# Two calls of the gate products round their weights' first part on ScalarE instead of GpSimd

## The chip, the cores and the metric

The kernel runs on one core of a Trainium2 chip, as one program with one launch. The metric is the time on the device in microseconds, the median of several executions. Five queues of instructions run beside each other: TensorE (PE, with its weight loads listed as PEld), VectorE (DVE), ScalarE (ACT), GpSimd (POOL) and SyncE (SP), which issues most of the DMAs.

## The reference, cut to what matters

One layer over 2048 latent tokens and 256 context tokens of width 1024. A modulated RMSNorm gives `h`; one input projection of it feeds two token mixers and the gates that multiply and merge what they give.

```python
h = _rmsnorm(x, norm_w) * (1.0 + scale[:, None]) + shift[:, None]
w_state, w_rest = w_in[:, :N_STATE], w_in[:, N_STATE:]
qkv, beta_r, decay_r, kb, vb = _split_cols(h @ w_state, STATE_SIZES)
za, qb, zb, ga, gb = _split_cols(h @ w_rest, REST_SIZES)   # za, zb: 512 columns; ga, gb: 1024
oa, _, _ = _gdn_bidir(qa, ka, va, g, bt, s_f, s_b, True)   # gated DeltaNet, both directions
ya = _gdn_output(oa, za, gdn_norm_w)                       # rmsnorm(oa) * silu(za)
ob = _latent_attention(...)                                # window of 128, 8 heads
yb = ob * jax.nn.silu(zb)
y = jax.nn.sigmoid(ga) * (ya @ w_proj_a) + jax.nn.sigmoid(gb) * (yb @ w_proj_b)
x = x + gate[:, None] * (y @ w_out)
```

The DeltaNet runs in chunks of a state recurrence, for each head, forwards and backwards:

```python
v_new = u_n - jnp.einsum('bhck,bhkv->bhcv', w_n, s)
s_new = s * jnp.exp(gl_n)[..., None, None] + jnp.einsum('bhck,bhcv->bhkv', kd_n, v_new)
o = jnp.einsum('bhck,bhkv->bhcv', qd_n, s) + jnp.einsum('bhij,bhjv->bhiv', qk_n, v_new)
```

## The kernel before, in words

All arithmetic is in float32. Where a product is large, each operand is split in two parts: a high part rounded to the format `fp32r`, and a low part, the rest that the rounding left. Three matmuls (L524 to L526: high by high, high by low, low by high) then make one product of nearly full precision. The high and low parts of `h` (`hh`, `hl`) stay in SBUF for a group of 512 tokens; there are four latent groups.

The gates `za`, `zb`, `ga`, `gb` have 24 feature tiles of 128 columns. `gates` (L824) goes through a list of tiles and, for each, through a list of token groups. For a tile, `weights` (L235) loads 1024 x 128 weights in two halves of 256 KB (`wr`, two buffers), makes the high part `wh` of each half with one cast of 128 x 512, and the low part `wl` with one subtraction on DVE (L246). The cast is made either by POOL (L245) or, with `by_act`, by ACT (L243). `wh` and `wl` have two buffers each, so a cast can be done once the last product that reads the tile two places before has run. A tile and a token group are 24 matmuls of 128 x 128 by 128 x 512 into one of three accumulators (`rps`), evicted by a tanh on ACT (L810) and, for `za` and `zb`, by one more product on DVE (L812), and stored. The next tile's weights are asked for after the first token group of the tile in hand (L831).

There are three places of such work. All 24 tiles of token groups 2 and 3 come first, with the casts on ACT (L838). The first 15 tiles of groups 1 and 0 (`BESIDE` = 15) run beside the scan: four tiles are written ahead of it (L1164) and eleven behind it (L1167). The last nine tiles of groups 1 and 0 come after the attention and keep their casts on POOL.

The scan (`scan`, L1060) has 18 steps, each for both directions. In a step, `chain` makes the product of the state with the keys (`ksps`, L1085), corrects `x` (L1087), multiplies by the merged triangular matrix (`vps`, L1091), scales on DVE (`v`, L1094) and updates the state by `sps` (L1103) with L1106 in the first step and L1109 later. `merge` (L976) prepares the matrix of the next step: transposes (`mtp`), a copy on ACT (L1011), products (`myp`, `mep`) and copies on ACT (L1019, L1025, L1026) into `mw`, `my` and `mx`, whose empty parts POOL clears (L984). `output` (L1114) makes `aps` (L1126) and `ops` (L1137) and combines them on DVE (L1134 or L1131, L1138); the direction that comes to a block second loads what the first stored (`osp`). `finalize` (L1038) normalizes the sum and multiplies it by the gate. On DVE the long solution of triangular blocks in `base` (L690 to L762) ends in the same stretch, and a last one, `base4` (L764), follows it in the same buffer `N`: loaded in part by DMA (L777), scaled (L779), copied into three more ranges of partitions by DMA (L784), and solved by 63 pairs of small operations (L789, L791), which stand in DVE's queue among those of the scan.

What sets the order: the program is written in Python loops, but a scheduler with a simulated timeline (`schedule_with_timeline_sim=True`) sorts the instructions of each engine, and the scan has a higher priority than what is written around it (L1165). Each engine then runs its own list in that order, and waits by semaphores. So the list of PE is one sequence of gate matmuls with the products of the scan set between them. From 898 us on the stretch is that of the fifteen tiles; their last products, the scan's last steps and the first attention blocks share the time up to about 1410 us.

Of the kernel before, what the change touches and what calls it, by code (L numbers as in the profile page):

```python
# [32 lines left out]
def hybrid(tc, ins, out, dbg=None, upto=9):  # L33
    nc = tc.nc
    V, S, G, T = nc.vector, nc.scalar, nc.gpsimd, nc.tensor
    ctx = ExitStack()
    with ctx:
        _hybrid(ctx, tc, nc, V, S, G, T, ins, out, dbg, upto)


def _hybrid(ctx, tc, nc, V, S, G, T, ins, out, dbg, upto):
# [9 lines left out]
    def mem(tag):  # L51
        if dbg is not None:
            print("MEM", tag, tile.free_sbuf_bytes_per_partition(tc))
# [744 lines left out]
    def rest(ev, m, by_act):  # L798

        col, dst, mm = ((C_ZA, zasp, m) if m < 4 else (C_ZB, zbsp, m - 4) if m < 8 else  # L800
                        (C_GA, gasp, m - 8) if m < 16 else (C_GB, gbsp, m - 16))
        w = weights(w_in[:, col + mm * 128:col + mm * 128 + 128], KT, by_act)
        return w, dst, mm

    def rest_run(ev, job, m, gi):
        w, dst, mm = job
        ps = acc([128, 512], name="rps")
        fm_dense(ps, w, hh[gi], hl[gi])
        t = ev.tile([128, 512], F32, name="rt", bufs=2)
        S.activation(t, ps, AF.Tanh, scale=0.5)  # L810
        if m < 8:
            V.scalar_tensor_tensor(t, t, 1.0, ps, op0=ALU.add, op1=ALU.mult)  # L812
        (dma if m < 8 else adma)(dst[gi][mm], t)

    BESIDE = 15
# [8 lines left out]
    def gates(ms, gis, beside=(), by_act=False):  # L824
        beside = iter(beside)
        job = rest(ev, ms[0], by_act)
        for i, m in enumerate(ms):
            for j, gi in enumerate(gis):
                rest_run(ev, job, m, gi)
                if j == 0:  # L830
                    nxt = rest(ev, ms[i + 1], by_act) if i + 1 < len(ms) else None  # L831
                    next(beside, None)
            job = nxt
# [195 lines left out]
    def scan_consts(pool):  # L1029
        gw = pool.tile([128, 1], F32, name="gw")  # L1030
        dma(gw, ins["gdn_norm_w"][0].rearrange("(p o) -> p o", o=1))
        V.tensor_scalar(gw, gw, 0.5, None, op0=ALU.mult)
        al2 = pool.tile([128, NB, H], F32, name="al2")
        V.tensor_tensor(al2, alpha, alpha, op=ALU.mult)
        V.tensor_scalar(al2, al2, 1.0 / 128, None, op0=ALU.mult)
        return gw, al2
# [123 lines left out]
    with tc.tile_pool(name="scan", bufs=1, side="right", reuse_waits="tile") as scp:  # L1160
        scl_ = tc.tile_pool(name="scan2", bufs=1, reuse_waits="tile")
        scl = scl_.__enter__()
        cs = scan_consts(scl)
        gates(list(range(4)), (1, 0))  # L1164
        with tc.high_priority(tc.cur_priority):  # L1165
            scan(scp, scl, cs)
        gates(list(range(4, BESIDE)), (1, 0))  # L1167
        mem("r1b")
        scl_.__exit__(None, None, None)
    bs2_.__exit__(None, None, None)  # L1170
# [196 lines left out]
```

## Time and profile before

| | |
|---|---|
| time, median of 3 runs (lowest to highest) | 2026.38 us (2021.74 to 2027.2) |
| the profiled execution | 2024.6 us |
| its span, first to last instruction | 2022.9 us |
| mean granted TensorE clock | 0.986 |
| busy share PE, DVE, ACT, POOL | 96%, 70%, 39%, 32% |
| gate matmuls (L524 to L526 on `rps`) | 768 each, 308.4 to 308.6 us each line |
| casts of weights on POOL (L245) | 72, 47.7 us |
| subtractions L246 on DVE | 120, 92.6 us |

All rows are of one profiled execution. A row of the timeline gives the start in microseconds from the span's start, the duration, the engine, the line of the program, the operation, its output and inputs with their shapes, and in brackets the time for which the engine had stood idle, with what released it. A row of the waits adds up such idle times for one line and one releaser. In the table by stretch each engine has its busy time and its count of instructions, and after POOL come the granted clock (1.00 is 2.4 GHz), the mean busy share of the DMA engines and what they moved in GB/s.

### The profile page before, as it was taken

How to read it: one execution, taken by the hardware profiler on the slowest of the kernel's cores; microseconds unless marked ns; L12 is line 12 of the kernel's file. 1: busy time of each engine (PE TensorE's matmuls, PEld its weight loads, DVE VectorE, ACT ScalarE, POOL GpSimd, SP SyncE). 2: the span in 40 equal slices, each digit the busy share in tenths (PEclk: the TensorE clock that was granted, in tenths of full speed). 3: DMA queues.
4: the chain of work that ended last, by engine and by line, in shares of the span. 5: the costliest groups of instructions: out<-in, count | busy, mean ns of one | idle time of the engine just before them, and what ended most of it. 6: DMA issues, size and time to landing. Idle time of an engine off the chain costs nothing. (4 is left out here: it accounts for less than half of the span.)

```text
span 2022.9 us, 32038 instructions
## 1 busy us (share of the span) xinstructions
PE 1943.7 (96%) x11043; PEld 1630.9 (81%) x11043; DVE 1413.3 (70%) x2774; ACT 786.9 (39%) x1975; POOL 656.8 (32%) x751
## 2 busy tenths in 40 slices
PE   6999999989999899999999999999989999999999
PEld 3888888779898778787788888878777888878887
DVE  7979766667776999999699556635676878743322
ACT  6755545554343322111122223325665656531100
POOL 1742210224542211004222234323555443442221
PEclk8999999999999999999999999999999999999999
DMA  7552326755447633528877777664455555365542
GB/s 259 168 138 85 95 88 159 198 151 163 143 144 190 164 115 109 144 86 234 206 222 213 219 230 218 196 190 156 146 167 173 183 161 169 113 190 181 181 146 94
DMA packets 375511, 333.11 MB, mean 165 GB/s; under 512 B 83833, under 2 KB 299185, under 8 KB 374709
## 3 DMA queue, kind: packets, MB, share of 16 engines
q1 hardware_dynamic: 347924, 288.59, 49.4%
q10 hardware_dynamic: 27424, 42.48, 5.9%
q8 instruction: 87, 1.43, 0.3%
q14 instruction: 76, 0.61, 0.1%
HBM read 220.28 MB, written 109.13 MB: 163 GB/s over the span
## 5 line engine op out<-in xcount | busy, mean ns | idle before, releaser
L524 PE MATMUL rps<-hh,wh 128*128 128x512 f32 x768 | 308.4, 402 | 6.4 <-DVE rt L812 5.1
L526 PE MATMUL rps<-hh,wl 128*128 128x512 f32 x768 | 308.6, 402 | 0.0
L525 PE MATMUL rps<-hl,wh 128*128 128x512 f32 x768 | 308.5, 402 | 0.0
L524 PEld LDWEIGHTS rps<-hh,wh 128*128 128x128 f32 x768 | 145.4, 189 | 41.8 <-DVE rt L812 5.5
L563 DVE SCALAR_TENSOR_TENSOR cacc<-y,cw,cacc 128x512 f32<-128x512 f32 (+1 forms) x224 | 162.3, 746 | 22.7 <-ACT cacc L561 18.6
L524 PE MATMUL lps<-hh,wh 128*128 128x512 f32 (+1 forms) x448 | 171.5, 383 | 0.3 <-ACT y L634 0.3
L525 PEld LDWEIGHTS rps<-hl,wh 128*128 128x128 f32 x768 | 145.4, 189 | 32.4
L526 PE MATMUL lps<-hh,wl 128*128 128x512 f32 (+1 forms) x448 | 171.4, 382 | 0.0
L526 PEld LDWEIGHTS rps<-hh,wl 128*128 128x128 f32 x768 | 145.4, 189 | 32.0
L525 PE MATMUL lps<-hl,wh 128*128 128x512 f32 (+1 forms) x448 | 171.2, 382 | 0.0
L938 DVE TENSOR_TENSOR pl<-pt,ph 128x512 fp32r<-128x512 f32 x156 | 105.4, 685 | 43.7 <-ACT ph L936 42.9
L936 ACT CAST ph<-pt 128x512 fp32r<-128x512 f32 x156 | 90.4, 585 | 112.2 <-PE pt L934 77.8
L910 DVE CUSTOM_DVE_ANT_0 pr<-sc,band,sk 128x640 f32<-128x640 f32 (+1 forms) x128 | 106.5, 862 | 33.8 <-PE sc L906 18.1
L810 ACT ACTIVATE rt<-rps 128x512 f32<-128x512 f32 x96 | 57.3, 597 | 176.2 <-PE rps L526 162.6
L749 DVE TENSOR_TENSOR N<-N,btmp 128x62 f32<-128x62 f32 (+30 forms) x124 | 116.8, 942 | 3.0
L920 POOL TENSOR_SCALAR pr<-pr,sm 128x640 f32<-128x640 f32 (+1 forms) x128 | 99.7, 800 | 56.5 <-DVE sm L918 40.9
L747 DVE TENSOR_TENSOR btmp<-N 128x62 f32<-128x62 f32 (+30 forms) x124 | 114.8, 926 | 3.1
L912 ACT ACTIVATE pr<-pr,sm 128x640 f32<-128x640 f32 (+1 forms) x128 | 104.0, 815 | 19.6 <-DVE sm L910 19.6
L1216 PE MATMUL pps<-yh,wph 128*128 128x512 f32 x256 | 105.2, 415 | 5.8 <-ACT yh L1198 4.3
L246 DVE TENSOR_TENSOR wl<-wr,wh 128x512 fp32r<-128x512 f32 x120 | 92.6, 787 | 24.6 <-POOL wh L245 22.3
L245 POOL TENSOR_SCALAR wh<-wr 128x512 fp32r<-128x512 f32 x72 | 47.7, 678 | 180.1 <-PE lps L525 97.1
L1217 PE MATMUL pps<-yl,wph 128*128 128x512 f32 x256 | 101.5, 397 | 0.0
(301 smaller groups left out, 4944.9 us busy)
## 6 DMA issues: line engine op xcount, KB each, us to landing
wr<-in_w_in_dram SPq DMA_DIRECT2D x120, 256.0 KB
kw<-Ksp SPq DMA_DIRECT2D x28, 384.0 KB
x<-vsp SPq DMA_DIRECT2D x36, 256.0 KB
k<-ksp SPq DMA_DIRECT2D x34, 256.0 KB
kT<-kTsp SPq DMA_DIRECT2D x34, 256.0 KB
wm<-in_w_mod_dram SPq DMA_DIRECT2D x16, 512.0 KB
xt<-in_x_dram SPq DMA_DIRECT2D x16, 512.0 KB
dtl<-Dsp SPq DMA_DIRECT2D x32, 256.0 KB
```

The lines of the kernel that those rows point to most:

```text
L524: T.matmul(ps, lhsT=wh[:, k], rhs=xh[:, k], start=k == 0, stop=False)
L525: T.matmul(ps, lhsT=wh[:, k], rhs=xl[:, k], start=False, stop=False)
L526: T.matmul(ps, lhsT=wl[:, k], rhs=xh[:, k], start=False, stop=k == kt - 1)
L563: V.scalar_tensor_tensor(a, y[:, t:t + n], cw[:, m, t:t + 1], a, op0=ALU.mult, op1=ALU.add)
L747: V.tensor_tensor(tv, A[:, m + 1:, m].unsqueeze(2).to_broadcast([h1 + n, r, m]), A[:, m, 0:m].unsqueeze(1).to_broadcast([h1 + n, r, m]), o ...
L749: V.tensor_tensor(A[:, m + 1:, 0:m], A[:, m + 1:, 0:m], tv, op=ALU.add)
L910: V.tensor_tensor_reduce(s_, ps[:, o:768], band[:, b0:b0 + W + 256], -0.125, sk[:, 1, hd:hd + 1], ALU.add, ALU.min, sm[:, h, 1:2])
L912: S.activation(s_, s_, AF.Exp, scale=-1.0, bias=sm[:, h, 1:2], accum_out=sm[:, h, 2:3])
L920: G.tensor_scalar(p[:, h, :W + 256], p[:, h, :W + 256], sm[:, h, 3:4], 1.0, op0=ALU.mult, op1=ALU.mult)
L938: V.tensor_tensor(pl, pt, f32(ph), op=ALU.subtract)
L1216: T.matmul(ps, lhsT=wh[:, k, ms], rhs=hs[k], start=k == 0, stop=False)
L1217: T.matmul(ps, lhsT=wh[:, k, ms], rhs=ls[k], start=False, stop=False)
```

## The change

The two calls of `gates` around the scan pass `by_act=True`. Nothing else is changed. In `weights` (quoted above) this takes the branch L243 instead of L245 for 15 tiles, two casts each.

```diff
         cs = scan_consts(scl)
-        gates(list(range(4)), (1, 0))
+        gates(list(range(4)), (1, 0), by_act=True)
         with tc.high_priority(tc.cur_priority):
             scan(scp, scl, cs)
-        gates(list(range(4, BESIDE)), (1, 0))
+        gates(list(range(4, BESIDE)), (1, 0), by_act=True)
```

Since the scheduler sorts by its own timeline, the lists of all engines are another order afterwards. Three places follow. The first is ACT's list at the scan's start, as a difference of the two lists (`+` is new); `rt` is the gate's eviction, `mw`, `my` and `mx` are the parts of the merged matrix for the second step.

```order
 L810 ACTIVATE rt<-rps 128x512 x2
 L1011 COPY mw<-mtp 128x512
+L243 CAST wh<-wr 128x512 x2
 L1019 COPY my_10262<-myp 64x256
+L243 CAST wh<-wr 128x512 x2
 L1025 ACTIVATE mw<-mep 64x4x64
 L1026 ACTIVATE mx_10246<-mep 64x4x64
 L810 ACTIVATE rt<-rps 128x512
 L1011 COPY mw<-mtp 128x512
+L243 CAST wh<-wr 128x512 x2
```

Two pairs of casts now stand among the copies of one merge, the second of them directly ahead of L1025, and the third pair behind the next merge's first copy.

The second place is DVE's list where the solution of `base4` (L789 and L791 by turns) and an early output of the scan (`oa_10561`, L1138) stand together, again as a difference.

```order
 L789 TENSOR_TENSOR btmp<-N,btmp 128x61
 L791 TENSOR_TENSOR btmp<-btmp 128x61
+L1138 TENSOR_TENSOR oa_10561<-ops,oa_10561 128x512
 L789 TENSOR_TENSOR btmp<-N,btmp 128x60
 L791 TENSOR_TENSOR btmp<-btmp 128x60
 L789 TENSOR_TENSOR btmp<-N,btmp 128x118
-L1138 TENSOR_TENSOR oa_10561<-ops,oa_10561 128x512
 L791 TENSOR_TENSOR btmp<-btmp 128x59x2
```

L1138 has moved ahead of three of the small products.

The third place is PE's list at the first product of the scan that reads a state (L1085 on `S_10219`), in the order before,

```order
 L1103 MATMUL sps<-v_10231,k_10221 128x128 x4
 L1016 MATMUL myp<-my_10262,moff_10250 64x64
 L1014 MATMUL myp<-mw,moff_10244 64x64
...
 L526 MATMUL rps<-hh_150,wl 128x512
 L524 MATMUL rps<-hh_150,wh 128x512
 L525 MATMUL rps<-hl_151,wh 128x512
...
 L1085 MATMUL ksps<-S_10219,kT_10295 128x128 x4
```

and in the order after:

```order
 L1016 MATMUL myp<-my_10262,moff_10250 64x64
 L1085 MATMUL ksps<-S_10219,kT_10295 128x128 x4
 L526 MATMUL rps<-hh_150,wl 128x512
 L524 MATMUL rps<-hh_150,wh 128x512
 L525 MATMUL rps<-hl_151,wh 128x512
```

Before, 21 gate matmuls stood between the last of the small products `myp` and L1085; now they stand behind L1085, so that 100 instead of 121 gate matmuls of the changed tiles are ahead of it.

## Rows read from the trace of the kernel before

**Rows 1.** the page's first part: engine, busy us, share of the span, instructions.

```profile
PE 1943.7 (96%) x11043; PEld 1630.9 (81%) x11043; DVE 1413.3 (70%) x2774; ACT 786.9 (39%) x1975; POOL 656.8 (32%) x751
```

**Rows 2.** table by stretch, 900 to 1220: length, engines, clock, DMA.

```profile
900.00:1220.00 320.00, 308.30 (x2174) 264.60 (x2173) 242.90 (x542) 70.36 (x203) 97.23 (x135) 0.98 0.76 215
```

**Rows 3.** PE's waits from 900 to 1410: total us, times, longest.

```profile
PE ksps L1085 <- DVE S L1109: 5.4, 2, 4.7
PE aps L1126 <- DVE oa L1138: 3.2, 1, 3.2
PE ops L1137 <- DVE oa L1131: 2.0, 1, 2.0
PE sps L1103 <- DVE v L1094: 1.8, 2, 1.3
PE rps L524 <- ACT rt L810: 1.3, 3, 0.7
PE fps L1055 <- DVE oa L1048: 0.5, 1, 0.5
```

**Rows 4.** DVE's timeline before 992: start, us, instruction, [idle <-releaser].

```profile
966.22 0.11 DVE L756 MEMSET N<- 128x64 f32 x1
986.81 4.41 DVE L779 TENSOR_TENSOR N<-N,btmp 32x4096 f32<-32x4096 f32 x1 [10.72 <-DMA N<-Nsp]
```

**Rows 5.** DVE's timeline, 1014 to 1017.

```profile
1014.37 0.26 DVE L789 TENSOR_TENSOR btmp<-N,btmp 128x63 f32<-128x63 f32 x1 [5.71 <-DMA N<-N]
1016.42 0.26 DVE L791 TENSOR_TENSOR btmp<-btmp 128x60 f32<-128x60 f32 x1
1016.71 0.28 DVE L789 TENSOR_TENSOR btmp<-N,btmp 128x118 f32<-128x118 f32 x1
```

**Rows 6.** DVE's timeline near 1173.

```profile
1173.45 1.13 DVE L1131 SCALAR_TENSOR_TENSOR oa<-aps,npre,oa 128x128 f32<-128x128 f32 x4 [6.41 <-DMA oa<-osp]
```

**Rows 7.** lines of cast and subtraction (min/median/max ns); L246, 897 to 1380.

```profile
L245 POOL TENSOR_SCALAR wh<-wr x72: 614/622/1222, 135.0 to 1404.4; 128x512 fp32r<-128x512 f32 x72
L243 ACT CAST wh<-wr x48: 603/619/623, 568.9 to 887.3; 128x512 fp32r<-128x512 f32 x48
L246 DVE TENSOR_TENSOR wl<-wr,wh x120: 673/684/1786, 135.8 to 1405.5; 128x512 fp32r<-128x512 f32 x120
L246 DVE TENSOR_TENSOR wl<-wr,wh 128x512 fp32r<-128x512 f32 x44 | 35.3, 819 | 17.4 <-POOL wh L245 17.4
```

**Rows 8.** PE's timeline of gate matmuls, first and last of ten.

```profile
902.67 0.40 PE L526 MATMUL rps<-hh,wl 128*128 128x512 f32 x1
...
904.77 0.40 PE L526 MATMUL rps<-hh,wl 128*128 128x512 f32 x1
```

**Rows 9.** PE's timeline at scan products, and DVE's first state copy.

```profile
947.85 1.28 PE L1085 MATMUL ksps<-S,kT 128*128 128x128 f32 x10
954.74 1.06 PE L1091 MATMUL vps<-x,mw 128*128 128x128 f32 x8
1017.77 2.08 PE L1126 MATMUL aps<-S,qT 128*128 128x128 f32 x8 [3.25 <-DVE oa L1138]
943.46 0.69 DVE L1106 COPY S<-sps 128x512 f32<-128x512 f32 x1
```

**Rows 10.** the table by stretch, slices of 10 us.

```profile
990.00:1000.00 10.00, 5.30 (x36) 4.53 (x34) 9.97 (x14) 0.76 (x2) 5.14 (x4) 0.69 0.53 147
1010.00:1020.00 10.00, 6.75 (x53) 6.08 (x52) 5.29 (x20) 0.37 (x1) 0.83 (x1) 0.89 0.97 265
1170.00:1180.00 10.00, 8.02 (x49) 6.57 (x48) 3.77 (x11) 3.08 (x13) 2.97 (x5) 0.83 0.83 241
```

**Rows 11.** timelines of POOL and ACT near 949, and POOL at 1019.

```profile
948.86 0.69 POOL L245 TENSOR_SCALAR wh<-wr 128x512 fp32r<-128x512 f32 x1 [1.08 <-DMA wr<-in_w_in_dram]
949.83 0.38 ACT L1025 ACTIVATE mw<-mep 64x256 f32<-64x256 f32 x1 [6.49 <-PE mep L1023]
1019.16 2.17 POOL L1078 TENSOR_TENSOR x<-x,rin 128x512 f32<-128x512 f32 x2 [11.46 <-DMA x<-vsp]
```

## The prediction, made before the changed kernel was run

> **What bounds the kernel now.** I read the page's shares first: TensorE (PE) is busy 96% of a span of 2022.9 us, the next engine, VectorE (DVE), 70% [rows 1]. So a change elsewhere counts only through PE's idle time. The change acts from the first gate of token groups 0 and 1, near 898 us, to the end of the fifteenth tile; after that a sorted order of gates, scan and first attention blocks ends near 1410. The table by stretch comes next: in the 320 us from 900 to 1220 PE is busy 308.3, DVE 242.9, ScalarE (ACT) 70.4 and GpSimd (POOL) 97.2 [rows 2]. ACT and POOL are both mostly idle there. Then PE's waits: from 900 to 1410 there are 14.2 us of them in all, 12.9 of those end on DVE, 1.3 on ACT's evictions; POOL and the casts are in none [rows 3]. Three waits make up most of it: 4.7, 3.25 and 2.0 us [rows 3, 9]. Last the timeline around these three. In the first, DVE stood 10.72 us before L779 until the load of N landed, ran L779 for 4.4 us, and only then came to the state update L1109 for which PE stood at L1085 [rows 4]. In the second DVE stood 5.71 us for the copy of N into the other partitions, then ran nine small products before L1138 [rows 5]. In the third it stood 6.41 us for the output that the other direction had stored (L1131) [rows 6]. All three are DVE's own queue behind a DMA.
>
> **The change part by part.** It takes 30 casts (15 tiles of two) off POOL and gives them to ACT. On POOL one takes 0.622 us (median), on ACT 0.619 [rows 7]: 18.7 us leave POOL, 18.6 us come to ACT.
> *POOL, minus 18.7 us.* What hides it is PE's own work: no PE wait of the stretch ends on POOL. The nearest is the 0.5 us before L1055, whose last releaser is DVE's L1048, itself fed by POOL [rows 3]. I take 0; the bound is a gain of 0.5.
> *ACT, plus 18.6 us.* The cast of a tile waits for the last product that reads the buffer of two tiles before, as it did on POOL, and in the new order each pair stands where that product has just been issued, mostly next to the eviction of the same group, which becomes ready one matmul later. A pair is 1.24 us. The eviction it delays has three accumulators ahead of it, that is two groups of 24 gate matmuls, and one matmul takes 2.10 us / 9 = 0.233 us [rows 8], so 11 us. The scan's copies behind a pair are needed 4 us or more later, which one place of the rivals below spells out. I take 0; without that cover a pair costs its 1.24 us, 18.6 in all, which no row comes near.
> *DVE.* The subtraction L246 that follows each cast averages 0.819 us in this stretch against a median of 0.684 overall, and stood 17.4 us for POOL's cast [rows 7]. If the difference were POOL's doing, 30 x 0.135 = 4.1 us of DVE work go. Most of that lies in DVE's idle time. It can reach the end only ahead of the first stall, where DVE is full up to the MEMSET L756 at 966.22, behind which N is stored and the next N loaded into its buffer [rows 4]. But there the tail of DVE's list waits for PE: the scan's first products L1103 have 96 gate matmuls ahead of them in both orders, so the state updates before L756 cannot move far. I take 0.7 us earlier, between 0 and 4.1.
> The Trainium skill (SBUF — State Buffer, section Who interferes with whom) says that a VectorE instruction with two SBUF inputs and a GpSimd one that reads SBUF lock each other out, while ScalarE waits for nobody. The 0.819 against 0.684 agrees with it; taken to its end the rule would give all of the 4.1 us to DVE, and 2020.5 if every bit of it counted. The rows above let only the 0.7 through.
> *Order.* The sorted order changes on every engine, and that is where the time can move. PE's total work is the same, so I count how many gate matmuls stand ahead of each of the three waiting products, from the first matmul of the changed tiles. Ahead of the L1085 of the first stall: 227 before, 229 now: 2 x 0.233 = 0.5 us of that wait is filled. DVE's list from L1012 to L1109 has the same instructions. From there to the L1126 of the second: 28 before, 29 now, 0.2 us; and DVE reaches L1138 behind six small products instead of nine, two of the three that it no longer waits for taking 0.26 and 0.28, so 0.8 us sooner [rows 5]: 1.0 us gained. Between the store and the reload of the third: 21 before, 19 now, so its wait grows by 0.5 us. A new narrow place is the first L1085 of the scan, with 100 gate matmuls ahead instead of 121: PE comes there near 947.85 - 4.9 = 942.9, and the state that it reads was copied at 943.46, behind a subtraction that now stands after the copy [rows 9]. It may wait half a microsecond, which only takes as much from the 4.7 us behind it.
> Sum: -0.7 - 0.5 - 1.0 + 0.5 = -1.7 us. The profiled execution took 2024.6 us (1.7 outside its span), so 2022.9 on its scale; it lies 1.8 under the median of the runs, 2026.4, on whose scale the sum gives 2024.7. I forecast 2024.
>
> **The rivals.**
> *Freed DVE and POOL close the stalls.* If N came 4.7 us sooner, the first two stalls would go, and with the third 4.7 + 3.25 + 2.0 = 10.0 us. The stalls also cost clock: in the slices that hold them the granted clock is 0.69, 0.89 and 0.83 [rows 10], between the two levels of 2.4 and 1.2 GHz, and the eight products behind the second take 2.08 us where a like set takes 1.06 [rows 9]; busy time of the slice by the missing share of the clock is 5.30 x 0.31 + 6.75 x 0.11 + 8.02 x 0.17 = 3.7 us. The time would be 2026.4 - 13.7 = 2013. For it: POOL's cast held DVE for 17.4 us. Against it: the N that DVE waits for comes by DMA [rows 4, 5], and its store needs L756, which hangs on PE.
> *ACT's casts hold the scan's copies; slower.* In the new order the second pair behind the scan's start stands ahead of L1025 and L1026, the last copies of the merge for the next step. Before, POOL's second cast of that tile waited 1.08 us for its weights and ended at 949.55; L1025 ran at 949.83 [rows 11]. Its reader on PE, L1091, started at 954.74 [rows 9], so with two copies of 0.38 us the slack is 954.74 - 949.83 - 0.76 = 4.1 us. If the second cast ends after 953.9, PE stands idle from there, a microsecond for each. DVE's subtraction that frees the buffer of the raw weights is later in the new list (behind the state's copy), and SP's queue is full of the scan's loads, so the load may be late; the longest DMA wait on POOL in the stretch was 11.46 us [rows 11]. At that length PE loses 11.46 - 4.1 = 7.4 us, and 1.6 us of clock as behind the first stall: 2026.4 + 9.0 = 2035. Against it: it is one place; later pairs come once in 48 gate matmuls, 11 us or more.
> *The new order opens other narrow places.* The scan has 18 steps of two directions, each with several products whose cover by gate matmuls is counted anew. One that becomes too short costs about what the longer wait of L1103 cost before, 1.3 us [rows 3]. Three or four more of them than now make 2027 to 2029 of the forecast, which is still no change. For it: the order differs from the first step to the last. Against it: as many places get more cover as get less.
>
> **How the numbers follow.** A measurement of this kernel can tell 0.3%, some 6 us, from no change: under 2020.3 is faster, over 2032.5 slower. The forecast and the last rival, both between 2020.3 and 2032.5, get 0.60. The first rival, or enough of it to save more than 6 us, gets 0.22. The second, alone or with clock loss at other places, gets 0.18. The range reaches to where each rival nearly ends, 2013 to 2035. The forecast's own range is 2020 to 2029.
>
> **What would show it.** In the changed profile L245 has 42 casts and L243 78, ACT gains 18.6 us and POOL loses as much between 900 and 1410, and the sum of PE's waits there stays between 9 and 17 us. Right is: the stall before L1085 near 990 is still there and no longer than 4.7, that before L1126 about 2.2, that before L1137 about 2.5. The forecast is wrong if a PE wait of over 3 us appears that ends on ACT (second rival), if the wait for N is gone (first), or if the PE busy time of the stretch differs by more than the clock can explain.

## The result, and the profile after

| | before | after |
|---|---|---|
| median of 6 runs each (lowest to highest) | 2026.61 us (2021.74 to 2027.4) | 2032.14 us (2029.49 to 2034.98) |
| the profiled execution | 2024.6 us | 2029.49 us |
| its span | 2022.9 us | 2027.6 us |
| mean granted TensorE clock | 0.986 | 0.983 |

The ratio is 1.0031, 95% interval 1.0018 to 1.0045: slower by 5.5 us. The interval lies above no change, with 0.3% inside it.

What was moved has moved. First the page's first part of the kernel after, in the columns of [rows 1], then its lines of cast and subtraction.

```profile
PE 1948.6 (96%) x11043; PEld 1631.3 (80%) x11043; DVE 1411.9 (70%) x2774; ACT 801.9 (40%) x2005; POOL 638.5 (31%) x721
```

```profile
L243 ACT CAST wh<-wr x78: 602/620/673, 570.0 to 1226.4; 128x512 fp32r<-128x512 f32 x78
L245 POOL TENSOR_SCALAR wh<-wr x42: 615/618/1054, 137.2 to 1415.3; 128x512 fp32r<-128x512 f32 x42
L246 DVE TENSOR_TENSOR wl<-wr,wh 128x512 fp32r<-128x512 f32 x48 | 37.3, 799 | 21.8 <-ACT wh L243 11.3 <-POOL wh L245 9.3 <-issue 1.2
```

There are 42 casts on POOL and 78 on ACT, with medians within 4 ns of those in [rows 7]. POOL is 18.3 us less busy and ACT 15.0 us more. The third row is that of the stretch 897 to 1420; in the same stretch of before the 48 subtractions took 38.6 us (mean 820 ns), so DVE gains 1.3 us.

The time went into PE's idle time. PE's waits of the kernel after from 900 to 1410 (us in total, times, longest), to set against [rows 3]:

```profile
PE ksps L1085 <- DVE S L1109: 5.6, 2, 4.5
PE fps L1055 <- DVE oa L1048: 4.4, 1, 4.4
PE sps L1103 <- ACT v L1099: 3.8, 1, 3.8
PE rps L524 <- ACT rt L810: 3.2, 5, 1.1
PE aps L1126 <- DVE oa L1138: 0.4, 1, 0.4
```

With four more of 0.7, 0.6, 0.2 and 0.2 us the sum is 19.1 us, against 14.2. Two waits are new or grown: L1055 for a multiplication on DVE (4.4, before 0.5), and L1103 for an eviction on ACT (3.8). Two have gone: L1126 fell from 3.2 to 0.4, and L1137 for L1131, 2.0 before, is not in the list. The waits for the gates' evictions (L810) grew from 1.3 to 3.2 us; they are 3.2 as well in two kernels below, e2 with the casts on POOL and e4, which is not slower.

The table by stretch shows where, and what the waits did to the clock: 900 to 1220 for [rows 2], 990, 1010 and 1170 for [rows 10], and the two slices of the new waits (1160 and 1280).

```profile
900.00:1220.00 320.00, 309.61 (x2193) 266.50 (x2192) 243.12 (x543) 83.69 (x229) 80.28 (x109) 0.97 0.76 217
990.00:1000.00 10.00, 5.50 (x36) 4.64 (x35) 9.97 (x14) 0.76 (x2) 4.66 (x4) 0.69 0.41 118
1010.00:1020.00 10.00, 9.64 (x73) 8.39 (x72) 5.48 (x20) 2.16 (x7) 1.64 (x2) 1.00 0.95 258
1160.00:1170.00 10.00, 8.51 (x49) 7.64 (x50) 3.99 (x12) 2.29 (x7) 3.21 (x3) 0.66 0.84 259
1170.00:1180.00 10.00, 10.00 (x82) 8.83 (x80) 6.62 (x18) 5.61 (x19) 1.05 (x2) 1.00 1.01 287
1280.00:1290.00 10.00, 5.62 (x36) 5.15 (x31) 5.33 (x13) 1.35 (x3) 4.69 (x8) 0.69 0.52 165
```

The same two slices of the kernel before:

```profile
1160.00:1170.00 10.00, 10.00 (x69) 8.66 (x69) 4.26 (x13) 2.22 (x6) 1.72 (x4) 1.00 1.04 282
1280.00:1290.00 10.00, 9.33 (x64) 7.49 (x63) 5.87 (x14) 2.61 (x11) 7.29 (x12) 1.00 0.75 238
```

The slice at 1280 has fallen from 64 matmuls at full clock to 36 at 0.69, that at 1160 from 69 to 49 at 0.66; the one at 1010 has risen from 53 at 0.89 to 73 at 1.00, and the one at 1170, where the third stall was, from 49 at 0.83 to 82 at 1.00. Up to 1220 PE did 19 matmuls *more* than before: by then the gains at 1010 and 1170 outweigh the loss at 1160, and what remains is lost at 1280.

There the order of POOL's list decides. After a scan output has its last sum, ACT squares it (L1043), POOL makes a scale of it in four steps of four columns (L1044, L1045, L72, L1047), DVE multiplies (L1048) and PE transposes (L1055). Timeline of the kernel after, ACT's last square first, then POOL, DVE and PE:

```profile
1277.70 0.19 ACT L1043 ACTIVATION_READ_ACCUMULATOR fjunk<-oa 128x1 f32 x1
1277.10 0.64 POOL L1122 TENSOR_SCALAR_AFFINE_SELECT qd<-qd 128x512 f32<-128x512 f32 x1 [0.24 <-DMA qd<-QDsp]
1278.90 2.04 POOL L1078 TENSOR_TENSOR x<-x,rin 128x512 f32<-128x512 f32 x2 [1.16 <-DMA x<-vsp]
1280.89 0.20 POOL L1044 TENSOR_TENSOR fss<-fss,al 128x4 f32<-128x4 f32 x1
1281.18 0.19 POOL L1045 TENSOR_SCALAR fss<-fss 128x4 f32<-128x4 f32 x1
1282.75 0.63 POOL L1122 TENSOR_SCALAR_AFFINE_SELECT qd<-qd 128x512 f32<-128x512 f32 x1 [1.37 <-DMA qd<-QDsp]
1283.35 1.01 POOL L72 TENSOR_TENSOR fss<-fss,expo 128x4 f32<-128x4 f32 x1
1284.43 0.20 POOL L1047 TENSOR_TENSOR fss<-fss,alpha 128x4 f32<-128x4 f32 x1
1284.67 1.08 DVE L1048 TENSOR_TENSOR oa<-oa,fss 128x512 f32<-128x512 f32 x1 [6.91 <-POOL fss L1047]
1285.90 1.08 PE L1055 MATMUL fps<-ident,oa 128*128 128x128 f32 x4 [4.38 <-DVE oa L1048]
```

The squares are done at 1277.9. POOL comes to the first step 3.0 us later, at 1280.89, since two products L1078 stand ahead of it that wait for loads, and between the second step and the third stands an L1122 that waits 1.37 us for one more. PE stands 4.38 us. The Trainium skill (Perfetto Trace Analysis, section Tensor Engine Instruction (MATMUL, LD_WEIGHTS)) calls ACT, DVE and GpSimd strict first-in-first-out queues; these rows agree, with a step whose input was there 3.0 us before it ran. The same step, the tenth of sixteen such chains, in the kernel before:

```profile
1287.98 0.20 POOL L1044 TENSOR_TENSOR fss<-fss,al 128x4 f32<-128x4 f32 x1 [0.42 <-ACT fjunk L1043]
1289.65 0.20 POOL L1047 TENSOR_TENSOR fss<-fss,alpha 128x4 f32<-128x4 f32 x1
1289.89 0.69 DVE L1048 TENSOR_TENSOR oa<-oa,fss 128x512 f32<-128x512 f32 x1 [1.78 <-POOL fss L1047]
1290.72 0.63 PE L1055 MATMUL fps<-ident,oa 128*128 128x128 f32 x4 [0.52 <-DVE oa L1048]
```

The loads ahead of it had come by then, L1044 waited for the squares alone, the four steps followed each other, and PE stood 0.52 us. The difference of the waits is 4.4 - 0.5 = 3.9 us; PE's busy time in the slice by the missing clock is 5.62 x 0.31 = 1.7 us more. Together that is 5.6 us, an estimate from this one slice; e9 below measures the place at 6.6.

The second new wait is that of a cast, on the kernel after's ACT and PE:

```profile
1158.78 0.62 ACT L243 CAST wh<-wr 128x512 fp32r<-128x512 f32 x1 [7.00 <-DMA wr<-in_w_in_dram]
1159.30 0.58 ACT L1011 COPY mw<-mtp 128x512 f32<-128x512 f32 x1
1159.78 0.62 ACT L243 CAST wh<-wr 128x512 fp32r<-128x512 f32 x1
1160.30 1.14 ACT L1099 ACTIVATE v<-vps,br 128x128 f32<-128x128 f32 x4
1161.49 2.08 PE L1103 MATMUL sps<-v,k 128*128 128x128 f32 x8 [3.76 <-ACT v L1099]
```

The cast waits 7.00 us for weights whose load SP issued at 1154.28, behind the scan's loads; L1011 and L1099 stand behind it, and PE waits 3.76 us for L1099.

From the gates' first eviction (L810) of the changed tiles to the last one of the kernel it is 915.01 to 1445.08 before and 914.74 to 1452.06 after: 7.25 us longer. Behind it the lists are the same, and from that eviction to the end it is 577.8 us before and 575.6 after (from 1420 on PE waits 17.9 and 14.4 us), which gives 2.25 us back; the spans differ by 4.7 us. That rest behind the eviction varies from 575.0 to 580.1 us over all profiles of this document, so part of any difference between two single executions comes from there.

### The profile page after: what moved, and what is told of

Same layout as the page of the kernel before. It is cut to its first block, busy times and chain, and to the rows that moved or that the text cites. A ratio compares the mean times of both kernels' runs of the same rounds, so it can differ in the third digit from the quotient of the medians.

```text
span 2027.6 us, 32066 instructions
## 1 busy us (share of the span) xinstructions
PE 1948.6 (96%) x11043; PEld 1631.3 (80%) x11043; DVE 1411.9 (70%) x2774; ACT 801.9 (40%) x2005; POOL 638.5 (31%) x721
## 4 chain that ended last, share of the span: by engine, by line
PE 75%; DMA 9%; DVE 7%; ACT 3%; issue 3%; SPq 2%; POOL 2%; DVEq 0%; ACTq 0%; POOLq 0%
PE rps L526 8%; PE rps L524 8%; PE rps L525 8%; PE lps L525 3%; PE lps L524 3%; PE lps L526 3%; PE ops L1301 3%; PE ops L1303 3%; PE ops L1302 3%; PE pps L1216 3%; PE pps L1218 3%; PE pps L1217 3%; PE pt L934 2%; DMA dtl<-Dsp 2%; PE tmps L366 2%
## 5 line engine op out<-in xcount | busy, mean ns | idle before, releaser
L810 ACT ACTIVATE rt<-rps 128x512 f32<-128x512 f32 x96 | 57.4, 598 | 137.2 <-PE rps L526 125.9
L912 ACT ACTIVATE pr<-pr,sm 128x640 f32<-128x640 f32 (+1 forms) x128 | 104.0, 815 | 18.7 <-DVE sm L910 18.5
L246 DVE TENSOR_TENSOR wl<-wr,wh 128x512 fp32r<-128x512 f32 x120 | 89.1, 760 | 29.1 <-POOL wh L245 14.4
L1218 PE MATMUL pps<-yh,wpl 128*128 128x512 f32 x256 | 102.4, 400 | 0.0
```

Source lines behind the costliest of these rows:

```text
L912: S.activation(s_, s_, AF.Exp, scale=-1.0, bias=sm[:, h, 1:2], accum_out=sm[:, h, 2:3])
L1218: T.matmul(ps, lhsT=wl[:, k, ms], rhs=hs[k], start=False, stop=k == 3)
```

## The experiments

The change does two things at once: it gives casts to another engine, and it makes the scheduler sort every list anew. To part them, nine kernels hold the lists. From the first gate of the changed tiles on, a table gives each engine's list, and every instruction is queued behind the one before it by an edge that sets the order of issue and adds no wait:

```python
for s in steps:          # one engine's list
    i += s
    if last is not None:
        ...
        tc.add_manual_dep(ins[i], ins[last].name, no_wait, reason="hold_order")
    last = i
```

Ratios are to the kernel before on the same chip, with 95% intervals; they are not the quotient of the two medians, from which they differ by up to 0.0014. It took 2022.4 us (median) beside e1 to e4, 2021.9 beside e5 to e8 and 2026.0 beside e9 to e12, each four on a chip of their own.

### Engine and order apart

e1: the lists of before, the 30 casts taken out of POOL's and put into ACT's where the sorted order had them.

```diff
-        gates(list(range(4)), (1, 0))
+        gates(list(range(4)), (1, 0), by_act=True)
...
-        gates(list(range(4, BESIDE)), (1, 0))
+        gates(list(range(4, BESIDE)), (1, 0), by_act=True)
...
         hybrid(tc, aps, o)
+        hold_order(tc)
```

> The casts run on ACT as in the change, but every other instruction of all five engines keeps the list of the kernel before; in ACT's list the casts stand where the scheduler's list has them on POOL. Theory (a cast costs only where its weights land late and a scan step stands behind it in ACT's list): here the late pair, whose weights land near 1155, stands behind the copies L1099 of its step, so no PE wait over 1 us ends on ACT, the PE waits from 900 to 1410 stay near 14 us, and the time is that of before, 2024 to 2029. Rival 1 (ACT's queue is the cause in any order): a PE wait of 3 us or more ends on ACT between 1100 and 1210, and the time is 2030 to 2034. Rival 2 (freed POOL and DVE help once the order is held): 2018 to 2022.

2020.27 us, ratio 0.9989 (0.9976 to 1.0002). In its trace no wait of PE ends on a cast or on ACT's L1099. That profiled execution took 2025.98 us, the longest of the twelve: its stretch between the two evictions is 535.50 us, with 3.2 us before L1137 and 2.0 before L1055. So the old lists too can lose some 5 us in one execution, and it is the ratio over the twelve that shows no loss.

e2: the lists of after, the casts in POOL's (the two calls of `gates` as in the kernel before).

```diff
         hybrid(tc, aps, o)
+        hold_order(tc)
```

> The casts run on POOL as before, but every other instruction of all five engines keeps the list of the changed kernel. Theory: the wait of 3.76 us before L1103 that ended on ACT's L1099 near 1161 goes with its loss of clock, the waits that the new lists bring on their own (4.5 before L1085 near 995, 4.4 before L1055 near 1286) stay: 2025 to 2029. Rival 1 (all of the loss is the new order, whichever engine casts): 2030 to 2034, with a wait of 3 us or more near 1161 that ends elsewhere. Rival 2 (the engine alone): 2024 to 2027 and the wait before L1055 is under 1 us.

2032.82 us, ratio 1.0054 (1.0035 to 1.0073). Its long waits (PE's timeline):

```profile
994.32 2.07 PE L1085 MATMUL ksps<-S,kT 128*128 128x128 f32 x8 [5.08 <-DVE S L1109]
1164.36 2.00 PE L1126 MATMUL aps<-S,qT 128*128 128x128 f32 x8 [4.31 <-DVE oa L1138]
1287.09 1.08 PE L1055 MATMUL fps<-ident,oa 128*128 128x128 f32 x4 [5.50 <-DVE oa L1048]
```

The new engine with the old order is not slower, the new order with the old engine is. So the loss is the order's. The wait before L1055 is there with all casts on POOL, and the cast near 1160 holds the scan in this order wherever it runs: here through the subtraction L246, which waits 6.88 us for POOL's cast, and DVE's L1138 behind it, instead of through ACT's L1099.

### Which piece of the order

e3: the lists of after, with the pair of casts near 1160 moved behind what it held (ACT's list).

```diff
 L1099 ACTIVATE v_11741<-vps,br 128x128 x4
-L243 CAST wh<-wr 128x512
 L1011 COPY mw<-mtp 128x512
-L243 CAST wh<-wr 128x512
 L1099 ACTIVATE v_11779<-vps,br 128x128 x4
+L243 CAST wh<-wr 128x512 x2
```

> The changed kernel, all lists held, with one edit: the pair of casts that waited 7.0 us for its weights near 1152 stands behind the two groups of L1099 and the copy L1011 instead of among them. Theory: the wait of 3.76 us before L1103 is gone, the slice from 1160 to 1170 has its clock back (0.66, some 2 to 3 us), 2025 to 2028. Rival (the weights' lateness itself costs PE the time, wherever the cast stands): the wait moves to a gate matmul L524 or to L810 and the time stays at 2030 to 2034.

2028.58 us, ratio 1.0028 (1.0017 to 1.0038). The wait of L1103 has gone and nothing is won. PE's timeline shows what came instead:

```profile
1159.69 2.08 PE L1126 MATMUL aps<-S,qT 128*128 128x128 f32 x8 [2.28 <-DVE oa L1138]
1283.18 1.08 PE L1055 MATMUL fps<-ident,oa 128*128 128x128 f32 x4 [6.00 <-DVE oa L1048]
```

The casts' load still holds the subtractions on DVE, with L1138 behind them. The wait at L1055 is longer, since PE came to it 4.3 us earlier than in the change and DVE's L1048 ran only 2.7 us earlier.

e4: the same, and POOL's list with the four steps ahead of the instructions that wait for loads.

```diff
 L991 COPY mx_13109<-x_13111 64x4x64
-L1122 AFFINE_SELECT qd_13178<-qd_13178 128x512
+L1044 TENSOR_TENSOR fss<-fss,al_9877 128x4
+L1045 TENSOR_SCALAR fss<-fss 128x4
+L72 TENSOR_TENSOR fss<-fss,expo 128x4
+L1047 TENSOR_TENSOR fss<-fss,alpha 128x4
 L1078 TENSOR_TENSOR x_13221<-x_13221,rin 128x512
 L1078 TENSOR_TENSOR x_13246<-x_13246,rin 128x512
-L1044 TENSOR_TENSOR fss<-fss,al_9877 128x4
-L1045 TENSOR_SCALAR fss<-fss 128x4
+L1122 AFFINE_SELECT qd_13178<-qd_13178 128x512
 L1122 AFFINE_SELECT qd_13200<-qd_13200 128x512
-L72 TENSOR_TENSOR fss<-fss,expo 128x4
-L1047 TENSOR_TENSOR fss<-fss,alpha 128x4
```

> As the run with the pair later, and one edit of POOL's list near 1277: the four small steps of the norm (L1044, L1045, L72, L1047) stand ahead of the two L1122 that wait for their loads and of L1078, not among them. Theory: the wait of 4.38 us before L1055 that ended on DVE's L1048 falls under 2 us and the clock of that stretch (0.69 from 1280 to 1290) comes back: 4 to 6 us less than the run with the pair later, 2019 to 2024. Rival (L1048 was late for ACT's squares, not for POOL's place): the wait stays over 3 us and the time is that of the run with the pair later.

2020.27 us, ratio 0.9993 (0.9981 to 1.0005). The wait at L1055 has gone, and the stretch between the two evictions is 530.01 us, as before. e3 and e4 differ in POOL's list alone, ran on one chip, and their intervals lie apart.

e9: the lists of after with that one edit of POOL's, ACT's left as it was.

```diff
-L1122 AFFINE_SELECT qd_13178<-qd_13178 128x512
+L1044 TENSOR_TENSOR fss<-fss,al_9877 128x4
...
```

> The changed kernel, all lists held, with the edit of POOL's list near 1283 alone (the four small steps of the norm ahead of the two L1122 and of L1078); the late pair of casts stays where it was. Theory (of the loss only the wait before L1055 is lasting, the waits near 1160 take each other's place): the wait before L1055 under 1 us, the time back at that of before, 0.998 to 1.001. Rival (both new waits share the loss): 1.001 to 1.003, since the wait of 2 to 4 us before L1103 is still there.

2025.15 us, ratio 1.0005 (0.9989 to 1.0022). Timeline of POOL, DVE and PE at the edited place, and of PE at L1103:

```profile
1278.89 0.20 POOL L1044 TENSOR_TENSOR fss<-fss,al 128x4 f32<-128x4 f32 x1 [1.11 <-ACT fjunk L1043]
1280.54 0.20 POOL L1047 TENSOR_TENSOR fss<-fss,alpha 128x4 f32<-128x4 f32 x1
1280.77 1.51 DVE L1048 TENSOR_TENSOR oa<-oa,fss 128x512 f32<-128x512 f32 x1 [2.16 <-POOL fss L1047]
1282.42 0.63 PE L1055 MATMUL fps<-ident,oa 128*128 128x128 f32 x4
1161.71 2.08 PE L1103 MATMUL sps<-v,k 128*128 128x128 f32 x8 [3.75 <-ACT v L1099]
```

PE no longer stands at L1055, and the slice from 1280 has 80 matmuls at a clock of 1.00. The wait for the cast is all there, 3.75 us, and yet the stretch is 531.15 us instead of 537.32. The ratio's interval still overlaps that of the change (1.0018 to 1.0045), so the ratio alone does not decide. The traces do: PE's list is the same in the change and in e9, so the same two evictions of gates (L810) on either side of the place can be compared. First the change, then e9:

```profile
1281.55 0.60 ACT L810 ACTIVATE rt<-rps 128x512 f32<-128x512 f32 x1 [0.56 <-PE rps L526]
1303.73 0.60 ACT L810 ACTIVATE rt<-rps 128x512 f32<-128x512 f32 x1
```

```profile
1282.41 0.60 ACT L810 ACTIVATE rt<-rps 128x512 f32<-128x512 f32 x1 [0.56 <-PE rps L526]
1297.98 0.60 ACT L810 ACTIVATE rt<-rps 128x512 f32<-128x512 f32 x1
```

That is 22.2 us against 15.6. With POOL's list as sorted it is 22.8 in e2, 24.4 in e3 and 22.6 in e8, with the four steps moved 15.4 in e4. From the first eviction of the changed tiles up to this place the change takes 366.8 us, e9 367.2, e4 366.2 and e3 365.0; from the place to the last eviction each takes 148.3 to 148.4. So the loss of the stretch is the chain at L1055. The cast's wait, which the change and e9 share, can be no more of it than the 0.6 and 1.8 us by which e4 and e3 are shorter ahead of the place.

e8: the change as it is, no list held, beside e5 to e7.

```diff
-        gates(list(range(4)), (1, 0))
+        gates(list(range(4)), (1, 0), by_act=True)
...
-        gates(list(range(4, BESIDE)), (1, 0))
+        gates(list(range(4, BESIDE)), (1, 0), by_act=True)
```

> The changed kernel once more, beside the runs with held lists on the same chip. Theory (its loss is two waits of its own lists, which each execution has): 1.002 to 1.005 of the kernel before, a wait of 3 us or more before L1055 near 1286 and one of 2 us or more between 1155 and 1170. Rival (its loss was the chip's or the day's): a ratio whose interval holds 1.000.

2030.55 us, ratio 1.0029 (1.0013 to 1.0044); L1055 waits 5.20 us, L1103 2.05. The loss is there again, with the wait at L1055. Two of its eleven executions took 2020.86 and 2021.36 us, without any loss, so not each execution has it as expected; there is no trace of either.

### What the waits around 1000 and 1160 are worth

e5: the lists of e4, and on DVE the subtractions of those casts behind the scan's steps.

```diff
-L246 TENSOR_TENSOR wl<-wr,wh 128x512 x2
 L1138 TENSOR_TENSOR oa_11709<-ops,oa_11709 128x512
 L1109 SCALAR_TENSOR_TENSOR S_11751<-S_11587,tot,sps 128x128 x4
 L1109 SCALAR_TENSOR_TENSOR S_11789<-S_11625,tot,sps 128x128 x4
 L1018 TENSOR_TENSOR moff_11798<-myp,br 64x256
+L246 TENSOR_TENSOR wl<-wr,wh 128x512 x2
```

> As the run with the pair and POOL's steps moved, and one edit of DVE's list: the pair's two subtractions L246, which waited 6.3 us near 1157 for the late cast, stand behind L1138, the two state updates L1109 and L1018 instead of ahead of them. Theory (late weights hold whatever in-order list has their users ahead of a scan step): the wait of 2.58 us before L1126 that ended on DVE's L1138 goes under 0.5 and the clock of 1160 to 1170 (0.74) comes back, 3 to 5 us less than the run before, 0.9965 to 0.9980 of the kernel before. Rival (the gate products need these weights at once): the wait comes back at L524 or L526 and the ratio stays 0.9985 or more.

2024.46 us, ratio 1.0008 (0.9995 to 1.0021). L1126 no longer waits, but 12 us later L1137 does, for L1131. Nothing is won, against the theory. e6 and e7 let DVE run the state updates ahead of the product with N (L779) at the first stall, e6 in the lists of e5, e7 in those of before.

```diff
-L779 TENSOR_TENSOR N<-N,btmp 32x4096
 L246 TENSOR_TENSOR wl<-wr,wh 128x512 x2
...
 L1109 SCALAR_TENSOR_TENSOR S_10477<-S_10351,tot,sps 128x128 x4
 L1018 TENSOR_TENSOR moff_10486<-myp,br 64x256
+L779 TENSOR_TENSOR N<-N,btmp 32x4096
 L780 TENSOR_TENSOR N<-N,nb 32x4096
```

> As the run with the subtractions later, and one more edit of DVE's list: L779, which waits some 10 us for the load of N, stands behind the state updates L1109 and L1018 of its step. Theory: the wait of 4.8 us before L1085 near 993 and its loss of clock (0.55 from 990 to 1000) go, 5 to 8 us, 0.993 to 0.995 of the kernel before. Rival (N only comes later, and the copies and L789 behind it hold L1138 for longer): the wait before L1126 near 1015 grows by 3 us or more and less than 3 us are won, 0.996 or more.

2022.32 us, ratio 1.0005 (0.9993 to 1.0018).

> The kernel before, all lists held, with the same single edit: L779 behind the state updates L1109 and L1018 of its step. Theory: the wait of 4.7 us before L1085 and its clock go also where POOL casts, 0.996 to 0.9975 of the kernel before. Rival: the wait before L1126 (3.2) or before L1137 (2.0) grows by as much, 0.9985 or more.

2022.97 us, ratio 1.0004 (0.9993 to 1.0015). In both the first stall goes and the second grows, as the rivals had it; PE's timeline of e5 (to compare with), then of e6, then of e7:

```profile
996.92 2.08 PE L1085 MATMUL ksps<-S,kT 128*128 128x128 f32 x8 [3.90 <-DVE S L1109]
1173.03 2.08 PE L1137 MATMUL ops<-v,qd 128*128 128x128 f32 x8 [4.05 <-DVE oa L1131]
```

```profile
1014.27 2.08 PE L1126 MATMUL aps<-S,qT 128*128 128x128 f32 x8 [6.36 <-DVE oa L1138]
```

```profile
1013.21 2.08 PE L1126 MATMUL aps<-S,qT 128*128 128x128 f32 x8 [7.07 <-DVE oa L1138]
```

The stalls near 995 and 1015 are one chain, from the store and reload of N to the solution on DVE. Moving work ahead of its middle moves the wait to its end. What could shorten the chain is an earlier start. e12: the lists of e4 with the two loads of N moved up in SP's.

```diff
 L1118 DMA qT_10860<-qTsp 128x4x128
+L777 DMA N<-Nsp_89 16x4096
+L777 DMA N<-Nsp_90 16x4096
 L997 DMA moff_10650<-offsp_91 64x256
 L995 DMA mx_10646<-Xsp_0_95 64x4x64
...
 L813 DMA zasp_118<-rt 128x512
-L777 DMA N<-Nsp_89 16x4096
-L777 DMA N<-Nsp_90 16x4096
 L1077 DMA x_10736<-vsp 128x512
```

> As the run with the pair and POOL's steps moved, and one edit of SP's list: the two loads of N (L777) stand ahead of L997, L995 and L1082, right behind L1118. Theory (the two waits before L1085 and L1126 near 993 and 1014 are one chain, from the load of N through L779, L780, the copies and L789; only its start can shorten it): N lands 3 to 5 us sooner, the two waits fall by 3 to 5 us in sum and the clock with them, 0.996 to 0.998. Rival (the load is held by the store of N before it, or by the traffic, so its place in the list is nothing): L779 still starts near 983 to 986, 0.999 to 1.0005.

2021.34 us, ratio 0.9985 (0.9969 to 1.0000). Timeline of DVE and PE:

```profile
984.50 4.41 DVE L779 TENSOR_TENSOR N<-N,btmp 32x4096 f32<-32x4096 f32 x1 [7.73 <-DMA N<-Nsp]
993.62 1.51 PE L1085 MATMUL ksps<-S,kT 128*128 128x128 f32 x8 [2.43 <-DVE S L1109]
```

L779 starts 18.8 us behind the MEMSET L756 (965.70) instead of 21.2 in e4, whose lists it has otherwise, and PE's wait is 2.43 us instead of 4.83. The time does not show it clearly: the interval overlaps that of e4 (0.9981 to 1.0005), and the lead of 0.15% over the kernel before is at the edge of its own. That it is faster than the change as made (1.0013 to 1.0044 in e8) it owes at least in part to e4's edits.

### Half of the change

e10: no list held, only the four tiles ahead of the scan on ACT.

```diff
-        gates(list(range(4)), (1, 0))
+        gates(list(range(4)), (1, 0), by_act=True)
```

> The change of the first call alone (the first four tiles cast on ACT, the other eleven on POOL), sorted by the scheduler. Theory (each new sort draws the narrow places anew, the casts themselves cost nothing): anything from 0.997 to 1.004, and its difference from before is explained by PE waits from 900 to 1410 that end on DVE, not on ACT's casts. Rival (the casts ahead of the scan's start are what costs): 1.002 or more, with a wait that ends on ACT between 930 and 980.

2025.04 us, ratio 1.0003 (0.9988 to 1.0018).

e11: only the eleven tiles behind it.

```diff
-        gates(list(range(4, BESIDE)), (1, 0))
+        gates(list(range(4, BESIDE)), (1, 0), by_act=True)
```

> The change of the second call alone (tiles 5 to 15 cast on ACT, the first four on POOL), sorted by the scheduler. Theory: anything from 0.997 to 1.004, explained by PE waits that end on DVE; in POOL's list L1122 stands again between the last steps of a norm near 1285, but behind L1045 and L72. Rival (the casts beside the scan are what costs, whatever the sort): 1.002 or more, with waits of 2 us or more that end on ACT.

2023.01 us, ratio 0.9986 (0.9972 to 1.0001). In these two L1055 waits at most 0.7 and 1.9 us. In e10 a wait of 2.05 us before L1103 ends on ACT's L1099, but L1099 had itself waited for DVE's L1094, and no cast stood ahead of it. Neither half has the loss: it belongs to neither set of casts, but to the one order that both together gave.

## Why the prediction was wrong, point by point

- **POOL minus 18.7, taken as 0: right.** No PE wait of before was POOL's to give back.
- **ACT plus 18.6, taken as 0: right for the cost.** With the lists of before the casts on ACT cost nothing (e1, 0.9989). The cover of 11 us ahead of each eviction was too wide in the new order: PE waited 3.2 us in all for L810 instead of 1.3, but so it did in e2 with the casts on POOL.
- **DVE 0.7 us earlier: met in number, not shown as a gain.** L756 ran at 965.48 instead of 966.22 [rows 4]. But the first eviction of the changed tiles came 0.27 us earlier too. Counted from that eviction, L756 starts after 51.2 us in the kernel before, after 50.7 in the change and after 51.2 again in e4 and e9, whose lists there are those of the change. The bound of 4.1 us set a mean (0.819) against a median (0.684): the median in the stretch was 0.684 before as well, and its mean went from 820 to 799 ns. The 2020.5 is 2024.6 less 4.1 without the other terms; with them, on the scale of the medians, it would be 2021.3.
- **Order, the three old stalls: near at the first, off at the other two.** The first was forecast at 4.2 us and was 4.5. The second was forecast at 2.2 and was 0.4. The third was forecast at 2.5, and no wait of PE ends there: PE had already stood for the cast 10 us earlier. In e5, where that is taken away, the wait of L1137 is there with 4.05.
- **The step that failed is the sum of "Order".** It gave -1.0 of the forecast's -1.7 us, where the median rose by 5.5. It recounted the cover of three waits that were already there, and of the scan's first L1085. The new lists were treated as the old ones with other distances. They opened two narrow places, and the last rival, that named this, was priced by the longer wait of L1103 in the old trace, 1.3 us each. The one at L1055 was 4.4 us, 3.9 more than before, and some 1.7 us of clock; against the same lists with POOL's four steps moved (e9) the place takes 6.6 us more. Its size is not a matter of how many gate matmuls stand ahead, which is what was counted; it comes from what POOL's list had put into a chain that PE waits for: two products L1078 ahead of it, whose load was waited for 1.16 us and which ran 2.04, and an L1122 in its middle, with 1.37 and 0.63. The wait before L1055 was in the profile of before, with POOL named as its feeder, and "the bound is a gain of 0.5" was written beside it: POOL's list there was read for what it could give, not for what a new order could take.
- **The rival of the casts that hold the scan's copies: it happened, elsewhere, and was not the cost.** Near 949, where it was placed, the casts waited 3.64 and 1.42 us and PE not at all. It came at 1160 with the predicted mechanism and 3.76 us, but taking it away (e3) won nothing, and leaving it in (e9) lost nothing that can be measured. A "PE wait of over 3 us" that "ends on ACT" was given as the sign of this rival; the sign appeared and named the wrong cause.
- **The rival of the closing stalls** did not occur: L779 still stood 9.79 us for N.
- **The other signs.** The casts were 42 and 78, as said. The sum of PE's waits, which was to stay between 9 and 17 us, was 19.1. Between 900 and 1410 POOL lost 18.3 us and ACT gained 13.4.

Open: why two executions of the change were as quick as the kernel before, and why the loads in POOL's list landed as late as they did. No run held the lists of the change with nothing edited; but e2 and e3, which held their lists too, have the loss, and e1 and e7, which held those of before, do not.

## What to carry to other kernels

Where a scheduler sorts the lists, an edit that only changes an engine is two edits, and here the second was the larger: follow, in the new list of every engine, the small steps that the bound engine waits for, and look what load stands ahead of each. Holding the lists fixed parts the two in two runs. A wait that goes away buys nothing when what it waited for comes no earlier: the next one in the same chain takes its place.

## What the runs showed of the hardware

- *Two products on POOL took three times their length beside DVE.* In the kernel after, beside L779 (4.41 us), the two products L1078 took 6.18 us; at 1278.90 they took 2.04. The subtractions on DVE that overlap the end took 1.48 us each instead of 0.69.

```profile
986.33 4.41 DVE L779 TENSOR_TENSOR N<-N,btmp 32x4096 f32<-32x4096 f32 x1 [9.79 <-DMA N<-Nsp]
986.91 6.18 POOL L1078 TENSOR_TENSOR x<-x,rin 128x512 f32<-128x512 f32 x2 [11.03 <-DMA x<-vsp]
990.67 2.96 DVE L246 TENSOR_TENSOR wl<-wr,wh 128x512 fp32r<-128x512 f32 x2
```

  All three are instructions with two inputs in SBUF; the Trainium skill (SBUF — State Buffer, section Who interferes with whom) says that such a DVE instruction contends with a GpSimd one that reads SBUF, and these rows agree. L246 sped up by only 21 ns on average when 30 casts left POOL in the change (820 to 799); with the lists held the difference is 31 ns (before 820, e1 789) and 57 (e2 856, the change 799). Other work of POOL still ran beside it, as here.
- *Where PE waits it loses more than the wait.* Behind 3.76 us of idle PE the eight products L1103 took 2.08 us (1.06 at 1156.67), and the granted clock of the slice was 0.66, between the levels of 2.4 and 1.2 GHz. In the end little of that is left: up to the place of L1055 e3, without this wait, takes 365.0 us and the change 366.8.
